# Two chunks of the SSD scan per TensorE turn, TensorE in written order, the state product in 64-column products

## The chip, the cores and the metric

The kernel runs on one core of one Trainium2 chip. The metric is the device time of one execution in microseconds; the time of a kernel is the median of its runs.

## The reference, cut to what is computed

The trunk has two layers of width 1024 over 1024 positions, in float32. Layer 0 is an SSD mixer (a chunked linear recurrence with a causal convolution before it), layer 1 a retention mixer. The change touches layer 0 alone. Its core, with 8 groups of 4 heads of 64 columns, a state of 128 and chunks of 128 positions:

```python
z, xbc, dt = _split(h @ w_in, (SSD_DI, SSD_CONV_DIM, SSD_HEADS))
xbc = silu(_causal_dwconv(xbc, conv_w, conv_b))
xs, bm, cm = _split(xbc, (SSD_DI, SSD_GROUPS * SSD_STATE, SSD_GROUPS * SSD_STATE))
...
a_cum = jnp.cumsum(a, axis=2)                       # inside a chunk
decay = jnp.exp(jnp.where(causal, a_t[..., :, None] - a_t[..., None, :], -jnp.inf))
cb = jnp.einsum("bclgn,bcsgn->bcgls", cc, bc)
y_diag = jnp.einsum("bcgels,bcsgep->bclgep", cb[:, :, :, None] * decay, X)
states = jnp.einsum("bclgn,bclgep->bcgepn", bc, X * to_end[..., None])
chunk_decay = jnp.exp(a_cum[:, :, -1])
# scan over chunks: state <- chunk_decay * state + states; prev is the state before the chunk
y_off = jnp.einsum("bclgn,cbgepn->bclgep", cc, prev) * jnp.exp(a_cum)[..., None]
y = (y_diag + y_off + d_skip * xs) * silu(z)
y = _rmsnorm(y by groups) @ w_out
```

## The kernel before, in words

Activations lie transposed: 128 channels on the partitions, 1024 positions along the free axis. Every projection takes a weight slice of 128 output channels and makes two **halves** of 512 positions. A half is 24 products of 512 columns (lines L144 to L146: three products of a high and a low part in fp32r for each of 8 slices of the width), summed in one PSUM tile from a pool of three. Each group g needs ten or twelve halves: B, C, x0 and x1 (`ip`, with convolution: `acc` L345 and L347, tanh L349, `pre` L350) and the two gates z (`w`, L363 to L365). A generator yields between halves.

The scan of a group walks 8 chunks c. `front(g, c)` puts into one PSUM tile `pa` the transposes of x0 and x1 (L410), of B (L411) and the product of B and C (L412), from which VectorE and ScalarE make `xdt`, `xde`, `bn`, `cbm` and the decay matrix `m` (in the tile `acb`, whose rows of cumulated decay come by DMA from the DRAM table `acd`; L428 is Relu, L431 Exp, L432 the product with `cbm`). `back(g, c)` makes the output of a chunk: four products of 64 columns in `py` (L445, one for each head, the "diagonal" part), two of 128 columns from the state S and C (L451), the product `pst` of `bn` and `xde` (L468) and the new state S (L475 on GpSimd, L471 or L476 on VectorE). The state's part is scaled by a second table `eab` in `tof` (L461) and added to `yT` by GpSimd (L465).

`merge` interleaves the scan of group g, the projections of group g+1 and the gates of g, and the norm of group g-1 (`nsq`, `pn` L507, L508, L509, L512) by their shares. The tile framework's scheduler then decides, by a simulation of its own, the order in which each engine issues; a wait holds everything behind it on its engine.

Tiles that matter: `acc` has two buffers, which the norm's squares `nsq` share; `pst` has one, `S` two.

Of the kernel before, what the change touches and what calls it, by code (L numbers as in the profile page):

```python
# [20 lines left out]
P = 128  # L21
T = 1024
# [126 lines left out]
class Layer0:  # L149
    def __init__(self, tc, cx):  # L150
# [10 lines left out]
        for g in range(SSD_G):  # L161
# [213 lines left out]

    def load_decay(self, g, q):
        nc, st = self.nc, self.S[g]
        if ("acb", q) in st:
            return
        tensor, off = self.acd  # L380
        acb = self.tile([P, 4, 4, P], "acb", 2, f"acb{g}_{q}")
        nc.sync.dma_start(
            acb.rearrange("p c h l -> p c (h l)"),
            bass.AP(
                tensor=tensor, offset=off + (q * 4 * SSD_H + g * 4) * P,
                ap=[[0, P], [SSD_H * P, 4], [1, 4 * P]],
            ),
        )
        eab = self.tile([P, 4, 2, P], "eab", 2, f"eab{g}_{q}")
        for h in range(4):  # L390
            j, hh = divmod(h, 2)
            nc.sync.dma_start(
                eab[hh * 64 : (hh + 1) * 64, :, j, :],
                bass.AP(
                    tensor=tensor, offset=off + (q * 4 * SSD_H + g * 4 + h) * P,
                    ap=[[0, 64], [SSD_H * P, 4], [1, P]],
                ),
            )
        nc.scalar.activation(eab, eab, AF.Exp)
        st["acb", q], st["eab", q] = acb, eab  # L400

    def front(self, g, c):
        nc, st, ident = self.nc, self.S[g], self.ident
        BT, CT, X = st[("B",)], st[("C",)], [st[("x", 0)], st[("x", 1)]]
        q, cc = divmod(c, 4)
        self.load_decay(g, q)
        cs = slice(c * P, (c + 1) * P)
        pa = self.ps.tile([P, 512], F32, tag="pa", bufs=2, name=f"pa{g}_{c}")
        for j in range(2):
            nc.tensor.transpose(pa[:, j * P : (j + 1) * P], X[j][:, cs], ident)  # L410
        nc.tensor.transpose(pa[:, 2 * P : 3 * P], BT[:, cs], ident)  # L411
        nc.tensor.matmul(pa[:, 3 * P :], BT[:, cs], CT[:, cs], start=True, stop=True)  # L412
        col = c * SSD_H + g * 4
        hv = lambda t: t.rearrange("p (h d) -> p h d", h=4)
        bc = lambda t: t[:, col : col + 4].unsqueeze(2).to_broadcast([P, 4, 64])
        xdt = self.tile([P, 256], "xdt", 2, f"xdt{g}_{c}")
        nc.vector.tensor_tensor(hv(xdt), hv(pa[:, :256]), bc(self.dth), ALU.mult)
        xde = bn = None
        if c < NC - 1:
            xde = self.tile([P, 256], "xde", 2, f"xde{g}_{c}")  # L420
            nc.vector.tensor_tensor(hv(xde), hv(pa[:, :256]), bc(self.wde), ALU.mult)
            bn = self.tile([P, P], "bn", 2, f"bn{g}_{c}")
            nc.scalar.copy(bn, pa[:, 2 * P : 3 * P])
        cbm = self.tile([P, P], "cbm", 2, f"cbm{g}_{c}")
        nc.vector.tensor_tensor(cbm, pa[:, 3 * P :], self.mask4, ALU.mult)
        m = st["acb", q][:, cc]
        for h in range(4):
            nc.scalar.activation(  # L428
                m[:, h, :], m[:, h, :], AF.Relu, scale=-1.0, bias=self.acum[:, col + h : col + h + 1]
            )  # L430
        nc.scalar.activation(m, m, AF.Exp, scale=-1.0)  # L431
        nc.vector.tensor_tensor(m, m, cbm[:, None, :].to_broadcast([P, 4, P]), ALU.mult)  # L432
        return xdt, xde, bn, m

    def back(self, g, c, fr):
        nc, st = self.nc, self.S[g]
        CT, X, yT = st[("C",)], [st[("x", 0)], st[("x", 1)]], st["yT"]
        xdt, xde, bn, m = fr
        state = st.get("state")
        q, cc = divmod(c, 4)  # L440
        cs = slice(c * P, (c + 1) * P)
        col = c * SSD_H + g * 4
        py = self.ps.tile([P, 512], F32, tag="py", bufs=2, name=f"py{g}_{c}")
        for h in range(4):
            nc.tensor.matmul(  # L445
                py[64 * (h % 2) : 64 * (h % 2) + 64, (h // 2) * P : (h // 2 + 1) * P],
                xdt[:, h * 64 : (h + 1) * 64], m[:, h, :], start=True, stop=True,
            )
        if state is not None:
            for j in range(2):  # L450
                nc.tensor.matmul(  # L451
                    py[:, (2 + j) * P : (3 + j) * P], state[:, j * P : (j + 1) * P], CT[:, cs], start=True, stop=True
                )
        for j in range(2):
            nc.vector.scalar_tensor_tensor(
                yT[j][:, cs], X[j][:, cs], self.dsk2[:, 2 * g + j : 2 * g + j + 1], py[:, j * P : (j + 1) * P],
                ALU.mult, ALU.add,
            )
        if state is not None:
            tof = self.tile([P, 2, P], "tof", 2, f"tof{g}_{c}")  # L460
            nc.vector.tensor_tensor(  # L461
                tof, py[:, 2 * P :].rearrange("p (j l) -> p j l", j=2), st["eab", q][:, cc], ALU.mult
            )
            for j in range(2):
                nc.gpsimd.tensor_tensor(yT[j][:, cs], yT[j][:, cs], tof[:, j], ALU.add)  # L465
        if c < NC - 1:
            pst = self.ps.tile([P, 256], F32, tag="pst", bufs=1, name=f"pst{g}_{c}")
            nc.tensor.matmul(pst, bn, xde, start=True, stop=True)  # L468
            s2 = self.tile([P, 256], "S", 2, f"S{g}_{c}")
            if state is None:  # L470
                nc.vector.tensor_copy(s2, pst)  # L471
            else:
                hv = lambda t: t.rearrange("p (h d) -> p h d", h=4)
                cd = self.cdb[:, col : col + 4].unsqueeze(2).to_broadcast([P, 4, 64])
                nc.gpsimd.tensor_tensor(hv(s2), hv(state), cd, ALU.mult)  # L475
                nc.vector.tensor_tensor(s2, s2, pst, ALU.add)  # L476
            st["state"] = s2

    def ssd(self, g):
        st = self.S[g]  # L480
        st["yT"] = [self.tile([P, T], "yT", 4, f"yT{g}_{j}") for j in range(2)]
        fr = self.front(g, 0)
        yield
        for c in range(NC):
            nx = self.front(g, c + 1) if c + 1 < NC else None
            self.back(g, c, fr)
            fr = nx
            if c == NC - 2 and g + 1 < SSD_G:
                self.load_decay(g + 1, 0)
            yield  # L490

    def norm(self, g, lo, hi):
# [25 lines left out]
    def run(self, tail, start):  # L518

        nc, cx = self.nc, self.cx  # L520
        self.load_x()
        self.split_x(0)
        self.dt_project(0)
        self.squares(0)
        first, second = self.units([("B", 0)]), self.units([("C", 0)])
        self.first_banks = [self.ps.tile([P, HALF], F32, tag="pa", bufs=2, name=f"fb{i}") for i in range(2)]
# [540 lines left out]
```

## Time and profile before

| | |
|---|---|
| median of 3 runs (lowest to highest) | 1759.96 us (1756.84 to 1761.56) |
| the profiled execution's own time | 1760.33 us |
| its span | 1758.5 us |
| TensorE busy | 1717.0 us, 98% |
| VectorE busy | 1088.2 us, 62% |
| ScalarE busy | 687.6 us, 39% |
| GpSimd busy | 192.2 us, 11% |
| mean granted TensorE clock | 0.995 |

Times are microseconds from the span's start. The profiled execution's time is 1.8 us above its span, and 0.4 us above the median. PE is TensorE, DVE VectorE, ACT ScalarE, POOL GpSimd. In lists of instructions a row gives the start, the busy time of the merged instructions, the engine, the line, the output and inputs, and their count; brackets hold the idle time before it and what released it. The scan of layer 0 lies between about 76 and 745 us.

### The profile page before, as it was taken

How to read it: one execution, taken by the hardware profiler on the slowest of the kernel's cores; microseconds unless marked ns; L12 is line 12 of the kernel's file. 1: busy time of each engine (PE TensorE's matmuls, PEld its weight loads, DVE VectorE, ACT ScalarE, POOL GpSimd, SP SyncE). 2: the span in 40 equal slices, each digit the busy share in tenths (PEclk: the TensorE clock that was granted, in tenths of full speed). 3: DMA queues.
4: the chain of work that ended last, by engine and by line, in shares of the span. 5: the costliest groups of instructions: out<-in, count | busy, mean ns of one | idle time of the engine just before them, and what ended most of it. 6: DMA issues, size and time to landing. Idle time of an engine off the chain costs nothing.

```text
span 1758.5 us, 21524 instructions
## 1 busy us (share of the span) xinstructions
PE 1717.0 (98%) x8158; PEld 1383.0 (79%) x8158; DVE 1088.2 (62%) x1889; ACT 687.6 (39%) x1106; POOL 192.2 (11%) x221
## 2 busy tenths in 40 slices
PE   8999999999999999999999999999999999999996
PEld 5777777777878787688878888888888888888885
DVE  7857876768686868877553266346615661666443
ACT  6455544544545455545331232133213321343422
POOL 3012222222222223300000000000000000000000
PEclk9999999999999999999999999999999999999998
DMA  4143232333332333465431102111101221344452
GB/s 178 52 117 87 82 97 62 104 68 105 72 96 73 97 89 103 152 222 194 150 120 48 49 19 88 38 53 57 54 30 54 66 67 46 98 142 143 147 183 74
DMA packets 91766, 166.07 MB, mean 94 GB/s; under 512 B 8592, under 2 KB 42000, under 8 KB 91664
## 3 DMA queue, kind: packets, MB, share of 16 engines
q1 hardware_dynamic: 90368, 162.49, 30.0%
q10 hardware_dynamic: 1296, 2.23, 0.3%
q8 instruction: 64, 1.05, 0.3%
q14 instruction: 38, 0.31, 0.1%
HBM read 139.38 MB, written 25.30 MB: 94 GB/s over the span
## 4 chain that ended last, share of the span: by engine, by line
PE 53%; DVE 3%; DMA 3%; ACT 2%; issue 1%; SPq 0%; DVEq 0%; ACTq 0%
PE o1p L146 3%; PE g L146 3%; PE g L144 3%; PE o1p L144 3%; PE g L145 3%; PE o1p L145 3%; PE v L144 3%; PE v L145 3%; PE v L146 3%; PE o0p L145 3%; PE o0p L146 3%; PE o0p L144 3%; PE k L145 2%; PE k L146 2%; PE k L144 2%; PE q L144 1%
## 5 line engine op out<-in xcount | busy, mean ns | idle before, releaser
L144 PE MATMUL ip<-hh,w0h 128*128 128x512 f32 x496 | 202.3, 408 | 0.0
L146 PE MATMUL ip<-hh,w0l 128*128 128x512 f32 x496 | 197.4, 398 | 0.0
L145 PE MATMUL ip<-hl,w0h 128*128 128x512 f32 x496 | 195.6, 394 | 0.0
L110 DVE TENSOR_TENSOR w1l<-w1r,w1h 128x1024 fp32r<-128x1024 f32 x48 | 58.4, 1223 | 148.8 <-ACT w1h L109 148.2
L347 DVE SCALAR_TENSOR_TENSOR acc<-pre,vec,acc 128x1024 f32<-128x1024 f32 x96 | 125.0, 1304 | 7.0 <-ACT acc L345 6.4
L465 POOL TENSOR_TENSOR yT<-yT,tof 128x128 f32<-128x128 f32 x112 | 105.8, 965 | 164.0 <-DVE tof L461 164.0
L428 ACT ACTIVATE acb<-acb,acum 128x128 f32<-128x128 f32 x256 | 77.0, 388 | 98.9 <-DMA acb<-acd 98.9
L912 POOL TENSOR_TENSOR h<-h,frs 128x512 f32<-128x512 f32 x2 | 2.9, 1486 | 1004.0 <-ACT frs L906 1004.0
L146 PEld LDWEIGHTS ip<-hh,w0l 128*128 128x128 f32 x496 | 93.7, 189 | 20.3 <-issue 0.7
L144 PEld LDWEIGHTS ip<-hh,w0h 128*128 128x128 f32 x496 | 93.7, 189 | 19.5 <-issue 1.1
L145 PEld LDWEIGHTS ip<-hl,w0h 128*128 128x128 f32 x496 | 93.7, 189 | 18.9 <-issue 0.3
L144 PE MATMUL z<-hh,w0h 128*128 128x512 f32 x256 | 103.4, 404 | 1.4 <-DVE w L363 1.4
L109 ACT CAST w1h<-w1r 128x1024 fp32r<-128x1024 f32 x48 | 50.0, 1050 | 138.2 <-PE q L145 52.5
L144 PE MATMUL o0p<-o0yh,o0h 128*128 128x512 f32 x256 | 100.8, 394 | 1.3 <-ACT o0yh L109 1.0
L146 PE MATMUL o0p<-o0yh,o0l 128*128 128x512 f32 x256 | 101.1, 395 | 0.5 <-DVE o0l L110 0.4
L144 PE MATMUL v<-w1h,h 128*128 128x512 f32 x256 | 101.5, 397 | 0.0
L145 PE MATMUL o0p<-o0yl,o0h 128*128 128x512 f32 x256 | 100.0, 391 | 1.5 <-DVE o0yl L110 1.5
L146 PE MATMUL o1p<-o1yh,o1l 128*128 128x512 f32 x256 | 100.1, 392 | 0.4 <-DVE o1l L110 0.4
L145 PE MATMUL v<-w1l,h 128*128 128x512 f32 x256 | 100.3, 393 | 0.0
L146 PE MATMUL z<-hh,w0l 128*128 128x512 f32 x256 | 100.1, 391 | 0.0
L145 PE MATMUL z<-hl,w0h 128*128 128x512 f32 x256 | 100.1, 391 | 0.0
L146 PE MATMUL v<-w1h,h 128*128 128x512 f32 x256 | 100.1, 391 | 0.0
(244 smaller groups left out, 4071.4 us busy)
## 6 DMA issues: line engine op xcount, KB each, us to landing
w0r<-w SPq DMA_DIRECT2D x48, 512.0 KB, 3.3
acb<-acd SPq DMA_DIRECT2D x16, 1024.0 KB, 8.6
o0r<-w0o SPq DMA_DIRECT2D x32, 512.0 KB, 3.4
o1r<-w1o SPq DMA_DIRECT2D x32, 512.0 KB, 3.3
eab<-acd SPq DMA_DIRECT2D x64, 128.0 KB, 9.2
o0yr<-ysp SPq DMA_DIRECT2D x32, 256.0 KB, 3.5
w1r<-w1qk SPq DMA_DIRECT2D x16, 512.0 KB, 3.4
w1r<-w1g SPq DMA_DIRECT2D x16, 512.0 KB, 3.3
```

Source lines behind the costliest of these rows:

```text
L109: nc.scalar.copy(hi, src)
L110: nc.vector.tensor_tensor(lo, src, hi.bitcast(F32), ALU.subtract)
L144: nc.tensor.matmul(ps, ahi, bhi, start=first, stop=False)
L145: nc.tensor.matmul(ps, ahi, blo, start=False, stop=False)
L146: nc.tensor.matmul(ps, alo, bhi, start=False, stop=last)
L347: nc.vector.scalar_tensor_tensor(acc, pre[:, j : j + T], cw(j), acc, ALU.mult, ALU.add)
L428: nc.scalar.activation(m[:, h, :], m[:, h, :], AF.Relu, scale=-1.0, bias=self.acum[:, col + h : col + h + 1])
L465: nc.gpsimd.tensor_tensor(yT[j][:, cs], yT[j][:, cs], tof[:, j], ALU.add)
L912: nc.gpsimd.tensor_tensor(r, r, rs, ALU.mult)
```

## The change

A **turn** (`visit`) now covers two chunks, v = 0 to 3 in each group. It issues on TensorE: the two `pst` (L461), the whole front of the next turn (`front_pe`: for both chunks two transposes L396, one L397, one product L398; for v = 3 that is the front of the next group), and then `py`: for each chunk and head one product of 64 columns from `m` (L485) and, if there is a state, one of 64 columns from the state and `ce` (L491), which adds to it in PSUM. `ce` is C times exp(acum) (an Exp on ScalarE, L436 on VectorE); it takes the place of `eab`, whose 64 loads go, and of `tof` and the GpSimd adds of L465. `acb`, `xdt`, `xde`, `bn`, `cbm` are made for two chunks at once; `pa` is one tile of two PSUM banks, `S` has three buffers. The first group's gates come later in the list of projections. From the first front to the second turn of the last group, TensorE runs in the order in which the program is written (`manual_schedule`); the other engines are still ordered by the scheduler.

```diff
-        self.steps = [[("B", 0), ("C", 0), ("z", 0, 0), ("x", 0, 0), ("x", 0, 1), ("z", 0, 1)]]
+        self.steps = [[("B", 0), ("C", 0), ("x", 0, 0), ("x", 0, 1), ("z", 0, 0)]]
...
-            self.steps.append(nxt + ([("z", g, 0), ("z", g, 1)] if g else []))
+            self.steps.append(nxt + ([("z", g, 0), ("z", g, 1)] if g else [("z", 0, 1)]))
...
-        eab = self.tile([P, 4, 2, P], "eab", 2, f"eab{g}_{q}")
-        for h in range(4):
-            j, hh = divmod(h, 2)
-            nc.sync.dma_start(
-                eab[hh * 64 : (hh + 1) * 64, :, j, :],
...
+        pa = self.ps.tile([P, 2, 512], F32, tag="pa", bufs=1, name=f"pa{g}_{v}")
+        for i in range(2):
+            cs = slice((2 * v + i) * P, (2 * v + i + 1) * P)
+            for j in range(2):
+                nc.tensor.transpose(pa[:, i, j * P : (j + 1) * P], X[j][:, cs], ident)
+            nc.tensor.transpose(pa[:, i, 2 * P : 3 * P], BT[:, cs], ident)
+            nc.tensor.matmul(pa[:, i, 3 * P :], BT[:, cs], CT[:, cs], start=True, stop=True)
...
+            nc.scalar.activation(ce[:, o:], m[:, o:], AF.Exp)
...
+            nc.scalar.activation(m, m, AF.Exp, scale=-1.0)
+        nc.vector.tensor_tensor(m, m, cbm[:, :, None, :].to_broadcast([P, 2, 4, P]), ALU.mult)
+        c2 = st[("C",)][:, 2 * v * P : (2 * v + 2) * P].rearrange("p (c l) -> p c l", c=2)
+        nc.vector.tensor_tensor(
+            ce[:, o:], ce[:, o:], c2[:, o:, None, :].to_broadcast([P, 2 - o, 4, P]), ALU.mult
+        )
...
+        for i, c in enumerate(grow):
+            nc.tensor.matmul(pst[:, i, :], bn[:, i, :], xde[:, i, :], start=True, stop=True)
...
+                nc.gpsimd.tensor_tensor(hv(s2), hv(state), cd, ALU.mult)
+                nc.vector.tensor_tensor(s2, s2, pst[:, i, :], ALU.add)
...
+        pa = self.front_pe(*nx) if nx else None
+        py = self.ps.tile([P, 2, 2, P], F32, tag="py", bufs=2, name=f"py{g}_{v}")
...
+                    nc.tensor.matmul(
+                        out[hh], xdt[:, i, h * 64 : (h + 1) * 64], m[:, i, h, :], start=True, stop=s is None
+                    )
...
+                        nc.tensor.matmul(
+                            out[hh], s[:, h * 64 : (h + 1) * 64], ce[:, i, h, :], start=False, stop=True
+                        )
...
-                nc.gpsimd.tensor_tensor(yT[j][:, cs], yT[j][:, cs], tof[:, j], ALU.add)
...
-        merge((self.decay(), 3), (self.units(self.steps[0][2:]), 8))
-        for g in range(SSD_G - 1):
-            lst = self.steps[g + 1]
-            gens = [(self.ssd(g), 9), (self.units(lst), 2 * len(lst))]
-            if g:
-                gens.append((self.norm(g - 1, 0, T), 4))
-            merge(*gens)
+        merge((self.decay(), 3), (self.units(self.steps[0][2:]), 2 * len(self.steps[0][2:])))
...
+        with self.tc.manual_schedule(engines={mybir.EngineType.PE}):
+            self.fr = self.front(0, 0, self.front_pe(0, 0))
+            for g in range(SSD_G - 1):
+                lst = self.steps[g + 1]
+                gens = [(self.units(lst), 2 * len(lst)), (take(vs, 4), 4)]
+                if g:
+                    gens.insert(0, (self.norm(g - 1, 0, T), 4))
+                merge(*gens)
```

How the order of instructions moves is shown at three places. In these rows a name is followed by the tile's group and part and a running number; `pre0` is x0 of group 0, `pre8` and `pre9` x0 and x1 of group 4, `ip1_0` the first half of x1 of group 0.

TensorE near the start, where `pcum` (the cumulated decay) follows a half, in the kernel before:

```order
L144 MATMUL ip0_1_547<-hh7_149,w0h3_415 128x512
L145 MATMUL ip0_1_547<-hl7_157,w0h3_415 128x512
L146 MATMUL ip0_1_547<-hh7_149,w0l3_416 128x512
L304 MATMUL pcum_580<-t_a_470,con_70 128x256
L306 MATMUL ptot_582<-t_a_470,ones_r_72 128x256
L144 MATMUL ip1_0_602<-hh0_142,w0h4_515 128x512
```

The same place in the changed kernel:

```order
L144 MATMUL ip1_0_522<-hh7_149,w0h3_414 128x512
L145 MATMUL ip1_0_522<-hl7_157,w0h3_414 128x512
L146 MATMUL ip1_0_522<-hh7_149,w0l3_415 128x512
L396 MATMUL pa0_0_677<-con_70,pre0_418 128x128
L304 MATMUL pcum_547<-t_a_466,con_70 128x256
L306 MATMUL ptot_549<-t_a_466,ones_r_72 128x256
L144 MATMUL ip1_1_562<-hh0_142,w0h3_414 128x512
```

The first transpose of x0 (its input is the finished convolution) now stands ahead of `pcum`, and `pcum` behind the first half of x1, where the z halves no longer come ahead of x.

TensorE in the last turn of group 3 (v = 3), where the front of group 4 (`pa4_0`) stands, in the changed kernel:

```order
L145 MATMUL z3_1_0_3090<-hl7_157,w0h27_3020 128x512
L146 MATMUL z3_1_0_3090<-hh7_149,w0l27_3021 128x512
L461 MATMUL pst3_3_3119<-xde3_3_2999,bn3_3_2997 128x256
L396 MATMUL pa4_0_3124<-con_70,pre8_2756 128x128
L396 MATMUL pa4_0_3124<-con_70,pre9_2886 128x128
L397 MATMUL pa4_0_3124<-con_70,pre20_2563 128x128
L398 MATMUL pa4_0_3124<-pre28_2689,pre20_2563 128x128
```

The same front in the kernel before:

```order
L145 MATMUL ip21_0_3461<-hl7_157,w0h28_3377 128x512
L146 MATMUL ip21_0_3461<-hh7_149,w0l28_3378 128x512
L410 MATMUL pa4_0_3488<-con_70,pre8_2969 128x128
L410 MATMUL pa4_0_3488<-con_70,pre9_3123 128x128
L411 MATMUL pa4_0_3488<-con_70,pre20_2745 128x128
L412 MATMUL pa4_0_3488<-pre28_2865,pre20_2745 128x128
```

It followed the next half of group 5 (`ip21_0`) and the last z half; now it stands two halves earlier, directly behind the `pst` of its own turn.

VectorE around the end of the convolution of x1 of group 4 (L350 on `pre9`) in the changed kernel:

```order
L350 SCALAR_TENSOR_TENSOR pre8_2756<-pre8_2756,acc8_2873 128x1024
L347 SCALAR_TENSOR_TENSOR acc9_2940<-pre9_2886,vec_69,acc9_2940 128x1024
L363 TENSOR_TENSOR w3_0_3024<-z3_0_1_3054,rstd0_135 128x512
L365 SCALAR_TENSOR_TENSOR w3_0_3024<-tz300_3050,w3_0_3024 128x512
L110 TENSOR_TENSOR w0l28_3086<-w0r28_3083,w0h28_3085 128x1024
L347 SCALAR_TENSOR_TENSOR acc9_2940<-pre9_2886,vec_69,acc9_2940 128x1024
L365 SCALAR_TENSOR_TENSOR w3_0_3024<-tz301_3079,w3_0_3024 128x512
L363 TENSOR_TENSOR w3_1_3089<-z3_1_0_3090,rstd0_135 128x512
L474 TENSOR_TENSOR S3_6_3121<-S3_6_3121,pst3_3_3119 128x256
L350 SCALAR_TENSOR_TENSOR pre9_2886<-pre9_2886,acc9_2940 128x1024
```

And in the kernel before:

```order
L476 TENSOR_TENSOR S3_6_3364<-S3_6_3364,pst3_6_3362 128x256
L432 TENSOR_TENSOR acb3_1_3072<-acb3_1_3072,cbm3_7_3341 128x512
L365 SCALAR_TENSOR_TENSOR w3_0_3238<-tz301_3330,w3_0_3238 128x512
L363 TENSOR_TENSOR w3_1_3381<-z3_1_0_3382,rstd0_135 128x512
L350 SCALAR_TENSOR_TENSOR pre9_3123<-pre9_3123,acc9_3214 128x1024
```

In both, L350 on `pre9` stands behind the state S of chunk 6; in the changed kernel the `pst` that this S adds is issued in the very turn that needs `pre9`.

## Rows read from the trace of the kernel before

**Rows 1.** The page: busy time of each engine, its share of the span, instructions.

```profile
PE 1717.0 (98%) x8158; PEld 1383.0 (79%) x8158; DVE 1088.2 (62%) x1889; ACT 687.6 (39%) x1106; POOL 192.2 (11%) x221
```

**Rows 2.** Waits on TensorE: total, times, longest.

```profile
PE pst L468 <- ACT bn L423: 10.8, 9, 2.5
```

**Rows 3.** Timeline of TensorE around two of these waits.

```profile
105.11 0.70 PE L468 MATMUL pst<-xde,bn 128*128 128x256 f32 x2 [2.52 <-ACT bn L423]
...
257.96 0.70 PE L468 MATMUL pst<-xde,bn 128*128 128x256 f32 x2 [1.87 <-ACT bn L423]
```

**Rows 4.** Windows behind them; the third number from the right is the clock.

```profile
105.10:109.20 4.10, 4.09 (x18) 3.11 (x19) 1.57 (x3) 2.14 (x6) 0.00 (x0) 0.58 0.54 177
...
258.20:262.70 4.50, 4.50 (x19) 3.17 (x19) 4.47 (x9) 2.57 (x4) 0.00 (x0) 0.62 0.11 16
```

**Rows 5.** Timeline of TensorE around the output products of one chunk.

```profile
353.42 0.39 PE L146 MATMUL ip<-hh,w0l 128*128 128x512 f32 x1
353.74 0.66 PE L445 MATMUL py<-acb,xdt 128*64 128x128 f32 x8
354.33 0.71 PE L451 MATMUL py<-pre,S 128*128 128x128 f32 x4
...
355.11 0.39 PE L145 MATMUL ip<-hl,w0h 128*128 128x512 f32 x1
```

**Rows 6.** Timeline of the first L445 products of a chunk, in two short windows.

```profile
303.65 0.44 PE L445 MATMUL py<-acb,xdt 128*64 128x128 f32 x4
...
303.65 0.55 PE L445 MATMUL py<-acb,xdt 128*64 128x128 f32 x6
```

**Rows 7.** Timeline of TensorE around a front without 64-column products.

```profile
114.78 0.39 PE L146 MATMUL ip<-hh,w0l 128*128 128x512 f32 x1
115.00 0.38 PE L410 MATMUL pa<-con,pre 128*128 128x128 f32 x2
...
117.87 0.39 PE L145 MATMUL ip<-hl,w0h 128*128 128x512 f32 x1
```

**Rows 8.** Timeline of TensorE near the start: the first products of two halves.

```profile
55.13 0.39 PE L144 MATMUL ip<-hh,w0h 128*128 128x512 f32 x1
...
60.57 0.39 PE L144 MATMUL ip<-hh,w0h 128*128 128x512 f32 x1
```

**Rows 9.** Timeline of VectorE near the start.

```profile
45.22 3.68 DVE L347 SCALAR_TENSOR_TENSOR acc<-pre,vec,acc 128x1024 f32<-128x1024 f32 x3
48.82 0.68 DVE L363 TENSOR_TENSOR w<-z,rstd 128x512 f32<-128x512 f32 x1
...
62.04 1.75 DVE L292 RECIPROCAL t_u<-t_u 128x256 f32<-128x256 f32 x1
```

**Rows 10.** Timeline of VectorE and ScalarE between the table and its first use.

```profile
84.68 0.41 DVE L319 COPY acT<-pacT 128x256 f32<-128x256 f32 x1
...
95.32 4.79 ACT L428 ACTIVATE acb<-acb,acum 128x128 f32<-128x128 f32 x16 [4.52 <-DMA acb<-acd]
```

**Rows 11.** Timeline of group 3's second half, TensorE, ScalarE and VectorE.

```profile
386.90 1.88 PE L507 MATMUL pn<-nsq,ones_r 128*128 128x512 f32 x4
...
391.64 1.04 ACT L109 CAST w0h<-w0r 128x1024 fp32r<-128x1024 f32 x1
...
397.85 1.06 ACT L509 ACTIVATE nsq<-nsq 128x1024 f32<-128x1024 f32 x1
...
398.95 2.48 DVE L512 SCALAR_TENSOR_TENSOR yT<-yT,vec,nsq 128x1024 f32<-128x1024 f32 x2
...
415.37 1.21 DVE L350 SCALAR_TENSOR_TENSOR pre<-pre,acc 128x1024 f32<-128x1024 f32 x1
...
422.16 0.38 PE L410 MATMUL pa<-con,pre 128*128 128x128 f32 x2
```

**Rows 12.** Lines L432 and L342: duration in ns, least/median/most.

```profile
L432 DVE TENSOR_TENSOR acb<-acb,cbm x64: 675/692/1105, 105.4 to 732.3; 128x512 f32<-128x512 f32 x64
...
L342 DVE TENSOR_TENSOR pre<-ip,rstd x62: 671/683/692, 43.2 to 646.7; 128x512 f32<-128x512 f32 x62
```

More of the change, by code (lines that the diff above doesn't have):

```diff
@@ L377, in load_decay @@
         nc, st = self.nc, self.S[g]
-        if ("acb", q) in st:
-            return
         tensor, off = self.acd
-        acb = self.tile([P, 4, 4, P], "acb", 2, f"acb{g}_{q}")
+        acb = st["acb", q] = self.tile([P, 4, 4, P], "acb", 2, f"acb{g}_{q}")
         nc.sync.dma_start(
@@ L402, in front, with front_pe @@
-    def front(self, g, c):
+    def front_pe(self, g, v):
         nc, st, ident = self.nc, self.S[g], self.ident
         BT, CT, X = st[("B",)], st[("C",)], [st[("x", 0)], st[("x", 1)]]
[L405 to L413, printed above, removed]
-        hv = lambda t: t.rearrange("p (h d) -> p h d", h=4)
[L415 to L433, printed above, removed]
@@ new lines, in front_pe, with front @@
+        for i in range(2):
[4 more added lines that the diff above has]
+            nc.tensor.matmul(pa[:, i, 3 * P :], BT[:, cs], CT[:, cs], start=True, stop=True)
+        return pa
+    def front(self, g, v, pa):
+        nc, tc, st = self.nc, self.tc, self.S[g]
+        q, cc = divmod(2 * v, 4)
+        n = 1 if v == NC // 2 - 1 else 2
+        bc = lambda t, k: (
+            t.rearrange("p (c h) -> p c h", c=NC)[:, 2 * v : 2 * v + k, 4 * g : 4 * g + 4]
+            .unsqueeze(3).to_broadcast([P, k, 4, 64])
+        )
+        hv = lambda t, k: t[:, :k, :256].rearrange("p c (h d) -> p c h d", h=4)
+        bn = self.tile([P, 2, P], "bn", 2, f"bn{g}_{v}")
+        cp = nc.scalar.copy(bn[:, :n, :], pa[:, :n, 2 * P : 3 * P])
+        xde = self.tile([P, 2, 256], "xde", 2, f"xde{g}_{v}")
+        nc.vector.tensor_tensor(hv(xde, n), hv(pa, n), bc(self.wde, n), ALU.mult)
+        xdt = self.tile([P, 2, 256], "xdt", 2, f"xdt{g}_{v}")
+        nc.vector.tensor_tensor(hv(xdt, 2), hv(pa, 2), bc(self.dth, 2), ALU.mult)
+        cbm = self.tile([P, 2, P], "cbm", 2, f"cbm{g}_{v}")
+        nc.vector.tensor_tensor(
+            cbm, pa[:, :, 3 * P :], self.mask4[:, None, :].to_broadcast([P, 2, P]), ALU.mult
+        )
+        m = st["acb", q][:, cc : cc + 2]
+        ce = self.tile([P, 2, 4, P], "eab", 2, f"ce{g}_{v}")
+        o = 0 if v else 1
+        with tc.issue_after(cp.ins if hasattr(cp, "ins") else cp):
+            nc.scalar.activation(ce[:, o:], m[:, o:], AF.Exp)
+            for i in range(2):
+                col = (2 * v + i) * SSD_H + g * 4
+                for h in range(4):
+                    nc.scalar.activation(
+                        m[:, i, h, :], m[:, i, h, :], AF.Relu, scale=-1.0,
+                        bias=self.acum[:, col + h : col + h + 1],
+                    )
+            nc.scalar.activation(m, m, AF.Exp, scale=-1.0)
+        nc.vector.tensor_tensor(m, m, cbm[:, :, None, :].to_broadcast([P, 2, 4, P]), ALU.mult)
+        c2 = st[("C",)][:, 2 * v * P : (2 * v + 2) * P].rearrange("p (c l) -> p c l", c=2)
+        nc.vector.tensor_tensor(
+            ce[:, o:], ce[:, o:], c2[:, o:, None, :].to_broadcast([P, 2 - o, 4, P]), ALU.mult
+        )
+        return xdt, xde, bn, m, ce
@@ new lines, in visit @@
+    def visit(self, k):
+        nc = self.nc
+        g, v = divmod(k, NC // 2)
+        nx = divmod(k + 1, NC // 2) if k + 1 < SSD_G * NC // 2 else None
+        if v % 2 == 0 and k:
+            gq, q = divmod(k // 2 + 1, 2)
+            if gq < SSD_G:
+                self.load_decay(gq, q)
+        if v == 0:
+            self.S[g]["yT"] = [self.tile([P, T], "yT", 4, f"yT{g}_{j}") for j in range(2)]
+        st = self.S[g]
+        xdt, xde, bn, m, ce = self.fr
+        X, yT = [st[("x", 0)], st[("x", 1)]], st["yT"]
+        hv = lambda t: t.rearrange("p (h d) -> p h d", h=4)
+        chunks = (2 * v, 2 * v + 1)
+        grow = [c for c in chunks if c < NC - 1]
+        before = {}
+        pst = self.ps.tile([P, 2, 256], F32, tag="pst", bufs=1, name=f"pst{g}_{v}")
+        for i, c in enumerate(grow):
+            nc.tensor.matmul(pst[:, i, :], bn[:, i, :], xde[:, i, :], start=True, stop=True)
+        state = st.get("state")
+        for i, c in enumerate(chunks):
+            before[c] = state
+            if c not in grow:
+                break
+            s2 = self.tile([P, 256], "S", 3, f"S{g}_{c}")
+            if state is None:
+                nc.vector.tensor_copy(s2, pst[:, i, :])
+            else:
+                col = c * SSD_H + g * 4
+                cd = self.cdb[:, col : col + 4].unsqueeze(2).to_broadcast([P, 4, 64])
+                nc.gpsimd.tensor_tensor(hv(s2), hv(state), cd, ALU.mult)
+                nc.vector.tensor_tensor(s2, s2, pst[:, i, :], ALU.add)
+            state = s2
+        st["state"] = state
+        pa = self.front_pe(*nx) if nx else None
+        py = self.ps.tile([P, 2, 2, P], F32, tag="py", bufs=2, name=f"py{g}_{v}")
+        for i, c in enumerate(chunks):
+            s = before[c]
+            for j in range(2):
+                out = [py[64 * hh : 64 * hh + 64, j, i, :] for hh in range(2)]
+                for hh in range(2):
+                    h = 2 * j + hh
+                    nc.tensor.matmul(
+                        out[hh], xdt[:, i, h * 64 : (h + 1) * 64], m[:, i, h, :], start=True, stop=s is None
+                    )
+                if s is not None:
+                    for hh in range(2):
+                        h = 2 * j + hh
+                        nc.tensor.matmul(
+                            out[hh], s[:, h * 64 : (h + 1) * 64], ce[:, i, h, :], start=False, stop=True
+                        )
+        cs = slice(2 * v * P, (2 * v + 2) * P)
@@ L466, in back @@
[L466 to L489, printed above, removed]
+                yT[j][:, cs], X[j][:, cs], self.dsk2[:, 2 * g + j : 2 * g + j + 1],
+                py[:, j].rearrange("p c l -> p (c l)"), ALU.mult, ALU.add,
+            )
@@ L490, in ssd, with visits @@
+        self.fr = self.front(*nx, pa) if nx else None
+    def visits(self):
+        for k in range(SSD_G * NC // 2):
+            self.visit(k)
             yield
@@ L525, in run @@
         first, second = self.units([("B", 0)]), self.units([("C", 0)])
-        self.first_banks = [self.ps.tile([P, HALF], F32, tag="pa", bufs=2, name=f"fb{i}") for i in range(2)]
+        fb = self.ps.tile([P, 2, 512], F32, tag="pa", bufs=1, name="fb")
+        self.first_banks = [fb[:, 0, :], fb[:, 1, :]]
         next(first)
```

46 lines of the change are left out of this document (8 added, 38 removed).

## The prediction

> **What bounds the kernel now.** I read the page first: of a span of 1758.5 us TensorE is busy 1717.0 [rows 1]. So time is won only by taking work or waits from TensorE, and lost by adding them. The list of waits came next. In layer 0 one kind stands out: `pst` waits for ScalarE's copy `bn`, nine times, 10.8 us in all [rows 2]. Then the timeline around those waits: two of them are 2.52 and 1.87 us long [rows 3], and in the windows behind these two the granted clock is 0.58 and 0.62 [rows 4], that is, TensorE spends part of the time at 1.2 GHz instead of 2.4. Last I read the timeline for what the small products cost between the halves, and walked the three places where the new order makes TensorE wait for something young.
>
> **What is removed.** *Small groups.* Between an L146 at 353.42 and the start of the second projection product behind the chunk's output, at 355.11, lie 1.69 us [rows 5]. A projection product takes 5.44/24 = 0.227 us, from two starts of halves [rows 8]. A 64-column product, which leaves two records, takes about 0.11 us: 2 more records add 0.11 [rows 6]. So the four of L445 are 0.43 us and the two of L451, four records of 0.11, 0.44. With two projection products of 0.227 that makes 1.32; 0.37 us is the price of entering and leaving such a group. A front without 64-column products has 3.09 us from 114.78 to 117.87 [rows 7] for 11 projection products (2.49) and five small records (0.55): 0.05 us for a break.
>
> In the order of the scan's part of the program I count 63 groups with 64-column products before and 33 now, and 127 breaks in the stream of projections before, 40 now. 30 x 0.37 = 11.1 us and 87 x 0.05 = 4.4 us are saved.
>
> The products themselves cost the same: one state product of 128 columns was 0.22, and two of 64 columns are 2 x 0.11. They now alternate with the diagonal ones in one group, and rows 6 show no price from one product to the next inside a group. The Trainium skill, "TensorEngine Tiling (Array Packing)", § Key Properties, says that a change of tiling mode makes TensorE drain, while a change of tile does not. By that rule all sixteen products of a turn, which have one tile shape, pay once; the sum would be the same. No run so far shows the alternating group.
>
> *Waits.* `pst` now uses a `bn` that was made a turn ago, three halves or 16.3 us earlier, so its 10.8 us go, and with them the two falls of the clock: 4.10 x 0.42 and 4.50 x 0.38 [rows 4], 1.7 us each, 3.4 together.
>
> Saved: 11.1 + 4.4 + 10.8 + 3.4 = 29.7 us.
>
> *At nothing:* the 64 loads of `eab`, the GpSimd adds and `tof`, and the added Exp and product for `ce`, lie on engines that are busy 62% or less [rows 1]; TensorE's three halves hide them, save where named below.
>
> **What is added.** *The start.* TensorE reaches the end of the second half after 49.5 at 60.57, as before [rows 8]. There now stands the transpose of x0, with `pcum` behind it; both wait for VectorE. I walked VectorE's new order with steps from rows: 1.20 for L347 (three in 45.22 to 48.82), 0.60 for half-width operations, 1.75 for the reciprocal [rows 9], 1.14 for L350 (1.21 less 0.07 of overlap [rows 11]). Three L347 end at 48.82; then L342, two L273, three L347 (5.4), L277, L350, L286, L342, L350, L110, L288 and L347 (6.0) bring it to 60.2. Then L342 on the half that has just ended (61.45), L347 (62.65), L291 and L292 (64.75), L347 (65.95), three small ones (67.2) and L350 (68.4). TensorE waits from 60.7 to 68.4: **7.7 us**, and, far longer than 2.52, with a fall of the clock, 1.7. Queued behind are `pcum`, which wants a `t_a` that ends 0.4 later and so costs little more, and every following half.
>
> *The first output.* In before the table's copy ended at 85.1 and the rows of `acb` reached ScalarE at 95.32 [rows 10]: 10.2 us by DRAM. In the new order the copy ends near 84.1 (behind the 7.7 us and one half more), so `acb` is there at 94.3. Behind it come the Exp for `ce` (0.6), eight Relu (half of 4.79), an Exp (1.06) and the product with `cbm` (1.2): 99.6. TensorE, with its halves, reaches the first `py` at about 96.4. **3.3 us**, 0.3 for the first state, and a fall of the clock, 1.7. Bounds 0 and 6, since two separate walks meet here.
>
> *The last turn of a group, seven times.* There TensorE issues `pst`, the transposes of the next group's x0, then of x1. VectorE's L350 on x1 stands behind the sum S of chunk 6, which needs this `pst`. Even with all else early, S (0.34, and 0.2 to reach it) and L350 (1.2) come after `pst`; TensorE has only the transpose of x0 to do: at least **1.75 us**. Before, L350 ended at 416.58 and the transposes came at 422.16 [rows 11], 5.6 us of slack.
>
> Whether x1 is later than that follows from the norm. `acc`, which x1 needs, is held by the norm's squares until L512 (now L527). From the start of `pn` at 386.90 to the end of L509 at 398.91 took 12.0 us [rows 11], with work of ScalarE's that now stands elsewhere; in the new order what lies from `pn` to there is L109, a table load, L523, L345, L523, a table load and L524, which in before took 7.3 us from L109's start at 391.64 [rows 11]. So P + 7.3, if P is the start of `pn`. Then VectorE has in its order two L527 (2.4, from 2.48 for two L512 [rows 11]), `xde`, `xdt`, `cbm` and two `yT` (2.1), four L347 (4.8), `ce` and `m` (2.3), two L350 (2.4), and five half-width operations, L110 and S (4.5): 18.4 us, x1 at P + 25.7. TensorE gets there after `pn` (1.7), turn 2 (4.0), three halves (16.3), `pst` and one transpose (0.5): P + 22.6. So I take **3.0 us** for six groups, and 2.4 for the first, which has no norm in it: 20.4. The stalls lie between 1.87 and 2.52 us or just above, where both falls of before lay [rows 3]; I take a fall in five of seven, 8.5 us.
>
> The durations in this walk are the undisturbed ones. L432, both inputs in SBUF, ranged from 675 to 1105 ns, while L342, with one input in PSUM, kept to 671 to 692 [rows 12]. The Trainium skill, "SBUF — State Buffer", § Who interferes with whom, says that a VectorE instruction with two SBUF inputs contends with a GpSimd operation that reads SBUF, and one with at most one does not. These rows agree; by the rule the walk can only lose the few GpSimd products that remain for S, and x1 would come a little earlier than by the means.
>
> **Sum.** Added: 9.4 + 5.3 + 20.4 + 8.5 = 43.6. Against the profiled execution's own 1760.3: 1760.3 - 29.7 + 43.6 = 1774.2; the median of the runs is 0.4 lower. Waits under 1 us of before, which also go, take about 2 more. I forecast **1772**.
>
> **Rivals.** *A, stalls without falls of the clock:* the 1.87-us idle shows a fall, but the stalls here follow a long dense stretch and may not. 1772 - 8.5 = 1763 to 1764. For it: 1.87 us is the shortest idle time with a fall that I have rows of, and the last turn's bound of 1.75 lies below it.
>
> *B, faster:* VectorE brings x1 as soon as S allows. The price is then 7 x 1.75 = 12.3 instead of 28.9, so 1755; with the first output on time (0 instead of 5.3) 1750. It decides if x1's last operation before S is ready by P + 23, that is, if VectorE's walk is 1.3 us shorter than mine. For it: the margin is small against a walk of 18 us. Against it: any gap on VectorE lengthens the walk, none shortens it.
>
> *C, slower still:* the last turns cost 4.5 us each because the norm's chain is late (7 x 1.5 = 10.5 more) with a fall each time (3.4): 1786. For it: in before the same chain took 12.0 us, not 7.3.
>
> *D, the change saves no small groups*, because a group's 0.37 is paid at each switch from diagonal to state product: 11.1 lost, 1783. Rows 6 speak against it.
>
> **How the numbers follow.** Forecast 0.42, A 0.18, B 0.27, C and D 0.13. A measurement of this kernel can tell 0.3%, 5.3 us, from no change: faster is below 1754.7, slower above 1765.2. B falls mostly below (0.23, 0.04 within); A mostly within (0.14, 0.04 above); the rest is above: faster 0.23, same 0.18, slower 0.59. The range reaches from B with both its gains, 1750, to C, 1787; the forecast's own range is 1766 to 1779.
>
> **What would show it.** In the list of waits `pst <- bn` is gone, and in its place stand transposes L396 waiting for L350: one of 7 to 8 us near 61, and seven of 1.8 to 4 us, one at the end of each group; then an L485 waiting for VectorE's L434 near 97. The windows behind them show a clock near 0.6 or 1.0, which tells the forecast from A. In a turn, sixteen 64-column products take about 1.8 us with 0.4 at the edges. I am wrong if x1 waits for S alone (B), if halves stretch between turns, or if turns 0 to 2 wait: there I found 1 to 2 us of slack for S and over 7 for `m`.

## The result and the profile after

The changed kernel takes 1780.0 us (median of 4 runs, 1772.87 to 1782.9) against 1758.4 for the kernel before in the same comparison: a ratio of 1.0116, 95% interval 1.008 to 1.0151. It is slower, as forecast, and 8 us slower than the forecast of 1772. The profiled execution took 1781.39 us with a span of 1779.6.

The page first: span, and busy time of each engine.

```profile
span 1779.6 us, 21284 instructions
...
PE 1715.4 (96%) x8382; PEld 1403.9 (79%) x8382; DVE 1086.1 (61%) x1681; ACT 697.1 (39%) x1066; POOL 100.8 (6%) x109
```

Against [rows 1] TensorE's busy time hardly moved (1717.0 to 1715.4) while the span grew by 21.1 us. So the loss is idle time. But busy time counts a product at the lower clock as longer, so it hides a saving as well. The waits of TensorE (total, times, longest) say where the idle time is:

```profile
PE pa L396 <- DVE pre L350: 30.0, 8, 9.3
...
PE py L485 <- DVE acb L434: 3.9, 1, 3.9
```

The wait of `pst` for `bn` [rows 2] is gone. Eight transposes wait for the end of a convolution instead. One is the 9.3 us near the start, seven are at the last turns. Here are both places on the timeline: first the start (TensorE, VectorE, ScalarE), then the last turn of group 3 (TensorE, VectorE).

```profile
69.61 0.47 PE L396 MATMUL pa<-con,pre 128*128 128x128 f32 x1 [9.31 <-DVE pre L350]
...
68.33 1.23 DVE L350 SCALAR_TENSOR_TENSOR pre<-pre,acc 128x1024 f32<-128x1024 f32 x1 [1.21 <-ACT pre L349]
...
65.95 1.28 ACT L349 ACT_TABLE_LOAD   x1 [5.52 <-DVE acc L347]
67.25 1.06 ACT L349 ACTIVATE pre<-acc 128x1024 f32<-128x1024 f32 x1
...
420.94 0.48 PE L396 MATMUL pa<-con,pre 128*128 128x128 f32 x1 [2.86 <-DVE pre L350]
...
402.37 2.68 DVE L527 SCALAR_TENSOR_TENSOR yT<-yT,vec,nsq 128x1024 f32<-128x1024 f32 x2
...
418.74 0.68 DVE L363 TENSOR_TENSOR w<-z,rstd 128x512 f32<-128x512 f32 x1
419.35 0.41 DVE L474 TENSOR_TENSOR S<-S,pst 128x256 f32<-128x256 f32 x1
419.67 1.22 DVE L350 SCALAR_TENSOR_TENSOR pre<-pre,acc 128x1024 f32<-128x1024 f32 x1
```

In the second place VectorE works without a gap from L527 at 402.37 on, and L350 on x1 ends at 420.89; the transpose starts at 420.94. In [rows 11] the same L350 had 5.6 us to spare. The other six waits of this kind are 2.45 us (group 0), four of 2.86, and 3.99 (group 6).

The windows that begin where these waits end (third number from the right: the granted clock) show a clock below 1.00, that is, part or all of the window at the lower of its two levels, except behind group 1's wait at 248:

```profile
69.60:75.80 6.20, 6.18 (x15) 4.78 (x16) 1.77 (x5) 0.80 (x2) 0.00 (x0) 0.50 0.01 3
102.90:106.50 3.60, 3.60 (x27) 3.08 (x28) 3.60 (x7) 3.41 (x9) 1.44 (x2) 0.53 0.37 132
160.90:164.60 3.70, 3.70 (x27) 3.48 (x29) 1.76 (x4) 1.62 (x5) 0.00 (x0) 0.54 0.00 0
248.10:252.00 3.90, 3.89 (x45) 3.47 (x46) 2.79 (x6) 2.64 (x9) 0.00 (x0) 1.00 0.00 0
333.70:338.60 4.90, 4.88 (x42) 4.43 (x43) 3.07 (x6) 3.60 (x11) 0.00 (x0) 0.65 0.02 3
420.90:424.00 3.10, 3.06 (x19) 2.83 (x21) 1.02 (x2) 0.83 (x3) 0.00 (x0) 0.51 0.00 0
507.90:512.70 4.80, 4.77 (x42) 4.32 (x43) 2.85 (x6) 3.49 (x11) 0.00 (x0) 0.64 0.00 0
595.10:601.50 6.40, 6.36 (x43) 5.72 (x44) 3.32 (x7) 4.10 (x11) 0.00 (x0) 0.51 0.01 3
684.80:690.20 5.40, 5.38 (x41) 5.16 (x41) 2.79 (x5) 3.16 (x10) 0.00 (x0) 0.50 0.00 0
```

Length times the missing share of the clock gives 3.1, 1.7, 1.7, 0, 1.7, 1.5, 1.7, 3.1 and 2.7 us, 17.2 in all, against 3.4 before [rows 4].

Two more falls lie behind waits outside these places. In layer 0's last projection TensorE waits 2.21 us for `o0yh`, until 754.64 (in the kernel before 0.99, until 713.81, and the clock stays at 1.00 behind it); the window there:

```profile
754.60:761.90 7.30, 6.50 (x15) 4.93 (x16) 6.60 (x9) 4.27 (x6) 0.37 (x1) 0.53 0.32 109
```

That fall costs about 3 us (7.30 x 0.47 is 3.4, of which some lies in a wait of 0.76). In layer 1 a wait of 1.87 us, until 935.22, is followed by a clock of 0.64 over 4.8 us, 1.7 us; the same wait of 1.87 in the kernel before, until 914.77, is followed by 1.00. With these two the falls come to about 22 us.

A turn without a wait, on TensorE, answers to [rows 5 to 7]. It is the first of group 4, whose first chunk has no state yet:

```profile
441.61 0.39 PE L146 MATMUL ip<-hh,w0l 128*128 128x512 f32 x1
441.83 1.02 PE L461 MATMUL pst<-xde,bn 128*128 128x256 f32 x4
...
443.89 0.88 PE L485 MATMUL py<-acb,xdt 128*64 128x128 f32 x12
444.60 0.39 PE L491 MATMUL py<-ce,S 128*64 128x128 f32 x4
444.81 0.39 PE L485 MATMUL py<-acb,xdt 128*64 128x128 f32 x4
445.03 0.39 PE L491 MATMUL py<-ce,S 128*64 128x128 f32 x4
445.35 0.50 PE L144 MATMUL ip<-hh,w0h 128*128 128x512 f32 x1
445.69 0.40 PE L145 MATMUL ip<-hl,w0h 128*128 128x512 f32 x1
```

Four records (two 64-column products) follow each other every 0.21 to 0.22 us, whether of L485 or of L491: the change from diagonal to state products costs nothing. The row with x12 holds the eight records of the first chunk and four of the second.

### The profile page after: what moved, and what is told of

It is laid out like the page before. It is cut to its first block, busy times and chain, and to the rows that moved or that the text cites. A ratio compares the mean times of both kernels' runs of the same rounds, so it can differ in the third digit from the quotient of the medians.

```text
span 1779.6 us, 21284 instructions
## 1 busy us (share of the span) xinstructions
PE 1715.4 (96%) x8382; PEld 1403.9 (79%) x8382; DVE 1086.1 (61%) x1681; ACT 697.1 (39%) x1066; POOL 100.8 (6%) x109
## 4 chain that ended last, share of the span: by engine, by line
PE 78%; DVE 11%; ACT 6%; DMA 3%; issue 1%; SPq 0%; DVEq 0%; ACTq 0%
PE ip L144 6%; PE ip L145 6%; PE ip L146 6%; PE o1p L146 3%; PE g L146 3%; PE g L145 3%; PE o1p L144 3%; PE g L144 3%; PE o1p L145 3%; PE v L144 3%; PE v L145 3%; PE v L146 3%; PE o0p L145 3%; PE o0p L146 3%; PE o0p L144 3%; DVE acc L347 2%
## 5 line engine op out<-in xcount | busy, mean ns | idle before, releaser
L144 PE MATMUL ip<-hh,w0h 128*128 128x512 f32 x496 | 196.8, 397 | 1.4 <-DVE pre L342 1.4
L347 DVE SCALAR_TENSOR_TENSOR acc<-pre,vec,acc 128x1024 f32<-128x1024 f32 x96 | 122.5, 1278 | 6.6 <-ACT acc L345 5.9
L109 ACT CAST w0h<-w0r 128x1024 fp32r<-128x1024 f32 x48 | 50.4, 1049 | 188.4 <-PE ip L145 157.9
L342 DVE TENSOR_TENSOR pre<-ip,rstd 128x512 f32<-128x512 f32 x62 | 42.6, 688 | 101.2 <-PE ip L146 101.1
L144 PE MATMUL g<-w1h,h 128*128 128x512 f32 x256 | 100.0, 391 | 0.0
L144 PE MATMUL o1p<-o1yh,o1h 128*128 128x512 f32 x256 | 99.6, 390 | 0.2 <-DVE vl L791 0.2
```

What stands on the lines that cost most here:

```text
L109: nc.scalar.copy(hi, src)
L144: nc.tensor.matmul(ps, ahi, bhi, start=first, stop=False)
L342: nc.vector.tensor_tensor(pre[:, 3 + h * HALF : 3 + (h + 1) * HALF], pt, self.rstd[:, sl], ALU.mult)
L347: nc.vector.scalar_tensor_tensor(acc, pre[:, j : j + T], cw(j), acc, ALU.mult, ALU.add)
```

## The experiments

My theory after the result: the regrouping saves what I counted; it is eaten by transposes that stand too early in TensorE's order for x1 (and x0 at the start), and by the falls of the clock behind those waits. Each median below is compared with the kernel before on the same chip.

**The output products ahead of the next group's front** (last turn of each group):

```diff
-        pa = self.front_pe(*nx) if nx else None
+        late = v == NC // 2 - 1
+        pa = self.front_pe(*nx) if nx and not late else None
...
+        if nx and late:
+            pa = self.front_pe(*nx)
```

> In the last turn of each group the output products py (about 2.1 us) are issued before the next group's front, so x1 has that much longer. My theory (TensorE waits 2.86 us at each of these places for L350 on x1, and the clock falls behind the idle time): the seven waits shrink from 20.7 us in all to about 6 (0.7 each, 1.9 in the last), none is long enough for a fall, so 14.5 us and the 13.6 us of the six falls go: about 1752 us against 1780. Rival, the clock falls because of the dense small products and not behind idle time: only the 14.5 go, 1766. Rival, the wait is for the state S and not for x1: S is as late relative to pst, so nothing moves but what py fills, and the wait appears at L491 in its place, 1775 or more.

Measured 1751.66 us (1750.96 to 1753.66), ratio 0.9946 (0.993 to 0.9963): the forecast of the theory. The waits:

```profile
PE pa L396 <- DVE pre L350: 9.7, 2, 9.3
PE py L492 <- DVE S L474: 5.1, 7, 1.7
```

The wait for x1 is gone but for 0.35 us in group 0, and a short one for the state S stands in its place, five times 0.58, once 0.5 and once 1.7. That is what remains of the floor through S that I had put at 1.75: `py` needs S of chunk 6 as well. Behind these waits the clock stays at its higher level. Moving the front behind `py` at seven places turns 1.2% slower into 0.5% faster than the kernel before.

**Useless products where TensorE idled:**

```diff
+        if v == 0 and g:
+            for i in range(13):
+                nc.tensor.matmul(
+                    pa[:, 0, :], self.hh[0][:, :P], self.hh[i % KT][:, :HALF], start=True, stop=True
+                )
```

> Thirteen products of 512 columns (2.95 us of TensorE work whose result is thrown away) stand ahead of the front of groups 1 to 7, where TensorE otherwise idles. It adds nothing useful and leaves x1 as late as it is. If the clock falls because TensorE idles: the idle time is replaced by work of about the same length (net +0.6 us, the last group still waits 1.1), and the six falls in the windows behind, 13.6 us, go: about 1767 us. Rival, the falls come from the load or from the small products: they stay, 1780 or a little more. That x1 is the thing waited for shows too: with 2.95 us of work ahead of it the wait must be near zero, not pushed back.

Measured 1770.22 us (1769.21 to 1771.66), ratio 1.0051 (1.0036 to 1.0066). With no useful work less, it is about 10 us faster than the changed kernel. The waits, and the windows of the filler and behind it in group 3:

```profile
PE pa L401 <- DVE pre L350: 10.3, 2, 9.3
```

```profile
414.90:418.40 3.50, 3.50 (x17) 2.80 (x16) 3.50 (x6) 1.70 (x2) 0.00 (x0) 1.00 0.46 150
418.40:423.00 4.60, 4.60 (x49) 3.97 (x48) 3.49 (x8) 3.23 (x10) 0.10 (x1) 1.00 0.07 22
```

The wait became work of the same length, x1 is as late as before, and the clock no longer falls, here or at the other six places. So these falls come from TensorE's idle time and not from the small products; that rival is out.

**The start alone, in written order:**

```diff
-        merge((self.decay(), 3), (self.units(self.steps[0][2:]), 2 * len(self.steps[0][2:])))
...
+            us, dec = self.units(self.steps[0][2:]), self.decay()
+            for gen in (us, dec, us, us, us, dec, us, dec):
+                next(gen)
```

> TensorE runs in written order from the decay on, with pcum behind the last half of x1 instead of the first, and no transpose of x0 ahead of it. My theory: the wait of 9.3 us near 60 goes with its fall (about 3.1 us), the table is made some 6 us earlier on the clock but TensorE is 11 earlier too, so the wait for m at the first py stays at 2 to 5 us: in all 10 to 14 us less than 1780, about 1767. Rival, the start is limited by VectorE's chain for dt and the table, so that the wait only moves to the first py or its front: 1775 to 1780.

Measured 1771.99 us (1766.16 to 1774.81), ratio 1.0056 (1.0035 to 1.0077): 8 us less than the changed kernel, under the 10 to 14 that I expected, and the ranges of the two overlap (1772.87 to 1774.81). The falls as a whole hardly shrank: the mean clock of the profiled run is 0.983 in both. In the waits the 9.3 us became 4.9 at `pcum`, since its input comes at 70.3 and one half more ends at 65.5; the wait for `m` at the first `py` stayed:

```profile
PE pcum L304 <- DVE t_a L298: 4.9, 1, 4.9
...
PE py L485 <- DVE acb L434: 3.4, 1, 3.4
```

**Every turn one half later:**

```diff
-                gens = [(self.units(lst), 2 * len(lst)), (take(vs, 4), 4)]
+                n = 2 * len(lst)
+                us = self.units(lst)
+                gens = [(us, evenly(n, n)), (vs, [3, 6, 9, 12] if g else [2, 5, 8, 10])]
...
-                    gens.insert(0, (self.norm(g - 1, 0, T), 4))
+                    gens.insert(0, (self.norm(g - 1, 0, T), evenly(4, n)))
...
+                merge_at(*gens)
```

Here `evenly` gives the positions that the halves had, and `merge_at` resumes the generators in the order of the positions; a 3 puts a turn behind the third half.

> Each turn comes one half later (behind 3, 6, 9, 12 halves of a group instead of 2, 5, 8, 11; in group 0 the last one stays two halves from x1), the front is still ahead of py. My theory: x1 then has 5.4 us more, against the 2.86 it is late, so the seven waits of 20.7 us and the 13.6 us of falls go: 1746 us, faster than the 1758 of before. The floor through S (1.75 us) goes too only if VectorE may run L350 on x1 ahead of S, which its new order decides; with the floor and no falls 1758. Rival, the norm is what is late and simply pushes the wait to the next place: a wait at the first turn of the next group, 1770 or more.

Measured 1736.44 us (1735.01 to 1738.62), ratio 0.986 (0.9845 to 0.9874), better than the 1746 that I expected. Of all the waits in the scan one is left, the start's:

```profile
PE pa L406 <- DVE pre L360: 9.3, 1, 9.3
```

The wait at the first `py` went too (3.9 us and its fall, which I had not taken off: group 0's first turn now stands one half later). The groups have become exactly periodic, which makes them a good measure: two starts of the norm's products `pn`, a group apart,

```profile
371.79 0.59 PE L532 MATMUL pn<-nsq,ones_r 128*128 128x512 f32 x1
...
454.34 1.02 PE L532 MATMUL pn<-nsq,ones_r 128*128 128x512 f32 x2
```

are 82.55 us from each other. In the changed kernel they are 87.22 (308.02 to 395.24):

```profile
308.02 0.59 PE L522 MATMUL pn<-nsq,ones_r 128*128 128x512 f32 x1
...
395.24 0.59 PE L522 MATMUL pn<-nsq,ones_r 128*128 128x512 f32 x1
```

82.55 + 2.86 (the wait) + 1.7 (the fall) is 87.1.

This change did one thing more than its expectation says: `pn` also moved, one half earlier among the halves. In the changed kernel it stands directly ahead of a `pst` (395.24 and 396.9), here two halves ahead of it (371.79 and 384.44). So from `pn` to the transposes of x1 there are now 33.5 us instead of 22.8, about 10.6 more and not 5.4, and L350 on x1 ends at 395.4, 9.9 us ahead of them. By the walk 5.4 would have covered the 2.86, but the turn's half alone was not run.

**Later turns and the new start together**, with `pcum` behind z's first half and the first group's turns behind 3, 5, 8 and 10 halves:

```diff
+            for gen in (us, dec, us, us, us, us, dec, us, dec):
...
-                gens = [(us, evenly(n, n)), (vs, [3, 6, 9, 12] if g else [2, 5, 8, 10])]
+                gens = [(us, evenly(n, n)), (vs, [3, 6, 9, 12] if g else [3, 5, 8, 10])]
```

> The turns one half later as in the run before, and the start in written order with pcum behind the first half of z (by then the input of pcum, which was ready at 70.4 in the run with only the start changed, is there) and the first turn behind three halves instead of two. My theory: the 9.3 us wait near 60 and the 3 to 4 us that its clock fall costs go, and the first output finds its decay rows in place: 1736 less 12 to 13, about 1724. Rival, the start is bound by VectorE and the table's way through DRAM, and the wait comes back at pcum, the front or the first py: 1730 or more.

Measured 1731.56 us (1729.73 to 1732.06), ratio 0.9832 (0.9816 to 0.9848). The start's wait is gone, but the rival was partly right. The table's rows reach ScalarE at 91.26, VectorE's queue behind it runs late, and the copy of the first state stands behind three operations of a convolution:

```profile
102.42 0.44 PE L501 MATMUL py<-ce,S 128*64 128x128 f32 x4 [3.26 <-DVE S L479]
...
100.76 1.27 DVE L357 SCALAR_TENSOR_TENSOR acc<-pre,vec,acc 128x1024 f32<-128x1024 f32 x1
101.95 0.41 DVE L479 COPY S<-pst 128x256 f32<-128x256 f32 x1
```

**The first state copied by ScalarE**, on top of that:

```diff
-                nc.vector.tensor_copy(s2, pst[:, i, :])
+                nc.scalar.copy(s2, pst[:, i, :])
```

> As the run with both the later turns and the new start, with the first state of each group copied from PSUM by ScalarE instead of VectorE. There TensorE waits 3.3 us near 99 for that copy, which stands on VectorE behind a delayed table of decay and three operations of 1.2 us of a convolution; on ScalarE it stands right behind an operation that ends near 97.4. My theory: the 3.3 us go and the fall of the clock behind them (1.7), 1732 less 5, about 1727. Rival, the place was only the first of several that are late because the decay rows come at 91: the wait moves to the next product (L501 of the same turn, or pst of the next), 1730 to 1732.

Measured 1728.33 us (1725.34 to 1730.29), ratio 0.9809 (0.9792 to 0.9827), the fastest version of this study. Both readings held in part: the 3.26 us went, and 1.5 us for S came back at the next turn. The range overlaps that of the run before, so the step from 1731.6 to 1728.3 is no more than likely.

**One more group of small products in 21 turns**, on top of the later turns (the second chunk's products one half after the first's):

```diff
+            if i and v < 3 and g < SSD_G - 1:
+                self.fr = self.front(*nx, pa)
+                nx = None
+                yield
...
-                gens = [(us, evenly(n, n)), (vs, [3, 6, 9, 12] if g else [2, 5, 8, 10])]
+                gens = [(us, evenly(n, n)), (vs, [3, 4, 6, 7, 9, 10, 12] if g else [2, 3, 5, 6, 8, 9, 10])]
```

> On top of the turns one half later: in turns 0 to 2 of groups 0 to 6 the products of the second chunk stand one half behind those of the first, which makes 21 more groups of 64-column products and leaves all else. It measures the main saving that I counted: at 0.37 us each, 7.8 us more than 1736, 1744; if a group costs only what any break in the stream of projections costs (0.05), 1737, and the gain of the change is not from fewer groups.

Measured 1745.51 us (1744.57 to 1746.32), ratio 0.9913 (0.9897 to 0.9928): 9.1 us more than 1736.44. The period of a group holds little else (the break that `pn` had for itself, 0.05 us by [rows 7], goes):

```profile
376.29 1.12 PE L537 MATMUL pn<-nsq,ones_r 128*128 128x512 f32 x2
...
459.93 0.70 PE L537 MATMUL pn<-nsq,ones_r 128*128 128x512 f32 x1
```

83.64 less 82.55 is 1.09 for three more groups, 0.363 us each. My 0.37 from [rows 5] was right.

**State products of 128 columns between the diagonal ones**, on top of the later turns:

```diff
-                    for hh in range(2):
-                        h = 2 * j + hh
-                        nc.tensor.matmul(
-                            out[hh], s[:, h * 64 : (h + 1) * 64], ce[:, i, h, :], start=False, stop=True
-                        )
+                    nc.tensor.matmul(
+                        py[:, j, i, :], s[:, j * P : (j + 1) * P], ce[:, i, 2 * j, :], start=False, stop=True
+                    )
```

> On top of the turns one half later: each pair of 64-column state products becomes one of 128 columns with the scaled C of the pair's first head (so the second head's state part is scaled by the wrong head's decay), added to the same PSUM region, directly between diagonal products of 64 columns. The TensorE time of the products alone is the same (0.22 against 2 x 0.11). If the price of a small group is paid at each change between the two product shapes, there are three more such pairs of changes in a turn whose chunks both have a state: 3 x 0.37 = 1.1 us for some 24 turns and 0.4 for the rest, about 30 us more, 1766. If it is paid only at the border to the projections, 1736.

Measured 1762.1 us (1761.47 to 1765.87), ratio 1.0015 (1.0006 to 1.0025): 25.7 us more than 1736.44, for the same product time. One pair on the timeline:

```profile
398.13 0.44 PE L495 MATMUL py<-acb,xdt 128*64 128x128 f32 x4
398.50 0.49 PE L499 MATMUL py<-ce,S 128*128 128x128 f32 x2
398.92 0.44 PE L495 MATMUL py<-acb,xdt 128*64 128x128 f32 x4
```

From one L495 to the next 0.79 us pass, where the 64-column form takes 0.43 (from 444.60 to 445.03 in the changed kernel): 0.36 for a change to the other shape and back. The period of a group says the same:

```profile
383.44 0.59 PE L530 MATMUL pn<-nsq,ones_r 128*128 128x512 f32 x1
...
469.53 0.59 PE L530 MATMUL pn<-nsq,ones_r 128*128 128x512 f32 x1
```

86.09 less 82.55 is 3.54 for ten more pairs of changes, 0.354 each. Adding into the same PSUM region is not what costs: in [rows 5] L445 and L451 write different regions, and the step between them takes 0.59 (353.74 to 354.33) instead of 0.43, 0.16 more; here it takes 0.37 (398.13 to 398.50) instead of 0.22, 0.15 more. The Trainium skill, "TensorEngine Tiling (Array Packing)", § Key Properties, has changing the mode drain TensorE and changing the tile not. These runs agree and give the price: about 0.36 us for each pair of changes, nothing between products of one shape.

## Why the prediction was right, and where it was off

**The sum's direction and its main terms held.** The waits were forecast by place, cause and size. At the last turns I had 3.0 us in six groups and 2.4 in the first, 20.4 in all; the trace has 2.86 in five, 3.99 in the sixth and 2.45 in the first, 20.7. That this wait is the distance between two walks the trace shows step by step: with `pn` at P = 395.24, the first L527 starts at P + 7.1 (I had 7.3), VectorE runs on for 18.5 us (18.4), x1 is there at P + 25.65 (25.7) and TensorE at P + 22.84 (22.6). Both runs that gave x1 more time took the wait away.

At the first output I had 3.3 and 0.3; measured 3.9, all of it for `m`, none for the first state. That is partly luck: `m` came at 102.8 instead of 99.6 and TensorE at 98.95 instead of 96.4, and the two errors nearly cancel.

**The start was 1.6 us too small.** The step "three small ones (67.2) and L350 (68.4)" left out that L350 waits for ScalarE's tanh L349, and that this tanh had to load its table first: 1.28 and 1.06 us after the last L347. L350 ended at 69.5, TensorE waited 9.3 instead of 7.7.

**The falls of the clock were mis-sized**, and this is the largest miss. I took seven behind the nine waits of the scan, 1.7 us each, 11.9 in all. There were eight, and three of them (the start, groups 5 and 6) cost 2.7 to 3.1: 17.2. Two more, at `o0yh` and in layer 1, I had at nothing, without a reason: about 22 in all, 10 more than in the sum. What the falls cost differs from run to run of one kernel: of the four runs of the changed kernel the fastest has a mean clock of 0.987 and the slowest 0.982, and span times the missing share is 23.0 and 32.1 us, which is most of the 10 us between them. Rival A, no falls, was wrong; the run with the filler shows that they hang on the idle time.

**The saving was larger than counted.** I had 29.7 and about 2 for small waits. The run with the later turns has a span of 1736.5, in which the start still costs 9.3 and a fall of about 3, and a fall of about 3 stands behind the wait for `o0yh` (2.12 us, until 713.16; clock 0.57 from 713 to 721): without them 1721, that is 37 under the 1758.5 of before. The price was confirmed (0.363 for a group, 0.354 and 0.36 for a pair of changes of shape). The remaining 5 to 6 us lie between the breaks, the order of the last group and the run's noise, and are not told apart. They took back half of what the falls cost more; that the forecast missed by 8 us only is partly due to this.

In sum the profiled spans should differ by 33.9 (the waits) + 22 (the falls) - 37 (the saving, with the old waits and falls in it) = 19 us; they differ by 21.1. Where the 2 us that are left go is open, and so is why the wait for `o0yh` grew.

Rivals B and C fell: VectorE was not 1.3 us early, and the norm's chain was not late. D is out by the turn of group 4 above: the alternating 64-column products pay nothing among themselves. The run with 128-column products shows what they would have paid.

The forecast that the few GpSimd products left would disturb VectorE less held too: L347, both of whose tensor inputs lie in SBUF, has a mean of 1304 ns in the page before and 1278 in the page after, and its longest went from 1682 to 1286 ns, where GpSimd is busy 100.8 us instead of 192.2 [rows 1]. This agrees with the rule of the Trainium skill, "SBUF — State Buffer", § Who interferes with whom, which I cited.

## What to carry to other kernels

An engine that runs in written order needs each consumer placed behind the time at which its producer ends, and not behind the place where the producer is issued. Here about 2 us more for x1 decided between 1.2% slower and 0.5% faster, and turns one half later, with `pn` one half earlier, made it 1.4% faster. Walk the producer's engine in its own order, with the small steps (a tanh, a table load), before fixing the position. And when a grouped stretch costs more than its products, look for the change of product shape: that was about 11 us of the saving here (30 groups at 0.363).

## What the runs showed of the hardware that I had not expected

A wait of 2.85 to 2.86 us was followed by a fall of the clock in groups 2 to 5 and by none in group 1 (0.51 to 0.65, and 1.00 in the windows above); idle time of that length cost from 0 to 3.1 us on top. In the kernel before, one wait of 1.87 us was followed by a fall (until 257.96, clock 0.62) and another of 1.87 by none (until 914.77, clock 1.00), so the forecast's count of five falls in seven was a guess. Filling TensorE's idle time with useless products was worth about 10 us in a kernel of 1780. The change between 64-column and 128-column products inside one accumulation costs as much, 0.36 us a pair, as entering and leaving a group from the projections.
